# Sums of weight blocks for two Winograd-form products: taken ahead, on POOL, in an earlier stage, and read back from HBM

## Chip, cores and metric

One core of one Trainium2 chip. The metric is the device time of one execution in microseconds, the median of several.

## What is computed

One layer of a hybrid encoder on x (1024 x 1024, float32). The parts that matter here:

```python
h = gate_a * (o_a @ w_branch_a[l]) + gate_b * (o_b @ w_branch_b[l])
x = layer_norm(DEEPNORM_ALPHA * x + h @ w_out[l], ln1_g[l], ln1_b[l])
up = causal_depthwise_conv(x @ w_up[l], conv_ffn[l])
a_ff, b_ff = jnp.split(up, 2, axis=-1)
x = layer_norm(DEEPNORM_ALPHA * x + (jax.nn.silu(a_ff) * b_ff) @ w_down[l], ln2_g[l], ln2_b[l])
```

`o_a` is a gated DeltaNet branch, `o_b` a spatial gating branch; `gate_a` and `gate_b` are sigmoids of columns of `x @ w_in`. w_up is 1024 x 5632, w_down 2816 x 1024.

## The kernel before

Every matrix product is made of three fp32r products of a high and a low part (`TERMS`). `split` (L111) makes the two parts: ScalarE copies the high part (L112), VectorE subtracts it (L113). One matmul is 128x128 by 128x512.

The program runs in stages, as TensorE sees them:

- To about 503 us: input projections, the DeltaNet solve and scan.
- Gate stage, 503 to 717 us: `mixed_b(d)` for d = 3 to 7 (L788), each a gate (L391, 48 matmuls, weights of 512 KB by `load_w`) and a branch (L461, 24 matmuls), then the gate A loop (L809), eight steps of the same size with gates of the next step ahead; `load_wo` brings blocks of w_out (L797). Raw weights go through two buffers (`wr`).
- w_out, 717 to 814 us: per row m of 128 tokens 48 matmuls (`wout_part`), then `wout_end`: residual sum and LayerNorm, whose reciprocal root is on POOL (L245, L246). Rows 0 and 1 are done in two halves of k, so that the blocks k = 4 to 7 are wanted late.
- Transition, 814 to 876 us: first products of the up projection, while the normalised x is transposed by TensorE (`to_b`, four 128x128 transposes to a group) into the operands B[1] to B[7].
- Up stage, 876 to 1280 us: x @ w_up by a Strassen-like scheme in Winograd's form. Columns are taken in 22 groups g of two 128-column blocks; each group has seven products (`up_product`, 12 matmuls). Products 1, 2 and 4 read blocks of w_up as they are; 5, 6, 7 and 3 read sums S of four blocks (`up_sums`, four POOL operations of 128x512, L942). `up_post` makes the convolution and the gating and stores F in HBM (`fd`, L1060). `order` is a fixed list, operands are split `LEAD` = 6 products ahead.
- Down stage, 1280 to 1562 us: F @ w_down by the same scheme, seven products for each of 11 block pairs j. The passes run in the order `PRODS` = 1, 5, 6, 3, 2, 7 (`dn_product`, 12 matmuls per step, L1204), and product 4 at the end from operands that stay in SBUF (L1308). Left sums (of F, `dn_left`, POOL) and right sums (of w_down, `dn_right`, POOL and VectorE in turn, L1156) are made on the way in planes `tt`, `b12`, `b22`, `b21`, `sa` of 11 x 512 columns, which `load_plane` fills from HBM. `finish` normalises and stores rows.

Each engine runs its instructions in the program's order, and SP issues its DMAs in the program's order: a DMA that waits holds up those behind it. Tiles come from pools with a number of buffers; who reuses a buffer waits for its last reader.

## Time and profile before

| | us |
|---|---|
| median of 3 runs | 1570.18 |
| lowest, highest | 1569.42, 1573.58 |
| profiled execution, own time | 1572.81 |
| its span | 1571.1 |
| TensorE busy in it | 1444.5 |
| VectorE busy | 1024.4 |
| ScalarE busy | 548.7 |
| POOL busy | 525.2 |

The profile is of one execution. Busy times are sums over the span; where an engine's idle time lies and what ended it is read from the views below. A DMA-issuing instruction of SP is not counted as busy.

### The profile page before, as it was taken

The page shows a single profiled execution, that of the slowest core. Times are in us where ns is not written, and L with a number is a line of the kernel's source. Part 1 is how long each engine was busy: PE and PEld are TensorE (multiplying, and loading weights), DVE is VectorE, ACT ScalarE, POOL GpSimd, SP SyncE. Part 2 cuts the span into 40 slices and gives each one's busy share as a digit, 9 for nine tenths or more (in the row PEclk, how much of TensorE's full clock was granted, in tenths as well). Part 3 has the DMA queues.
Part 4 walks back from the last instruction along what each step waited for, and adds up shares of the span by engine and source line. Part 5 has one row for each costly group of instructions (what it writes and reads, how often), then busy time and mean ns, then how long its engine had stood idle before and what let it go on. Part 6 is the DMA issues. An engine that isn't in the chain of part 4 may idle for free.

```text
span 1571.1 us, 17995 instructions
## 1 busy us (share of the span) xinstructions
PE 1444.5 (92%) x6807; PEld 1173.2 (75%) x6807; DVE 1024.4 (65%) x1556; ACT 548.7 (35%) x855; POOL 525.2 (33%) x491
## 2 busy tenths in 40 slices
...
POOL 2344353543531000000163233333333104790363
...
GB/s 231 20 36 41 28 15 39 28 27 28 28 14 41 40 54 65 78 60 198 56 67 55 80 81 67 81 84 84 88 68 79 91 153 394 194 121 107 128 100 54
DMA packets 124678, 129.75 MB, mean 83 GB/s; under 512 B 6267, under 2 KB 92975, under 8 KB 124591
## 3 DMA queue, kind: packets, MB, share of 16 engines
...
## 4 chain that ended last, share of the span: by engine, by line
PE 67%; DVE 17%; POOL 5%; DMA 4%; issue 4%; ACT 2%; SPq 0%; POOLq 0%; DVEq 0%; ACTq 0%
PE mm L990 21%; PE mm L391 18%; PE mm L461 6%; PE mm L867 5%; PE sm L990 3%; PE mm L1204 2%; DMA b<-in_w_down_dram 2%; PE sm L1308 2%; PE mm L239 2%; DVE op L113 2%; DVE u L606 2%; PE sm L1204 1%; DVE u L607 1%; DVE y L416 1%; DVE b L113 1%
## 5 line engine op out<-in xcount | busy, mean ns | idle before, releaser
L391 PE MATMUL mm<-xh,wh 128*128 128x512 f32 x1152 | 313.7, 407 | 0.0
L391 PEld LDWEIGHTS mm<-xh,wh 128*128 128x128 f32 x1152 | 213.3, 190 | 40.6 <-issue 0.4
L990 PE MATMUL mm<-xh,op 128*128 128x512 f32 x888 | 218.0, 396 | 6.0 <-DVE ca L1018 4.8
L990 PEld LDWEIGHTS mm<-xh,op 128*128 128x128 f32 x888 | 164.5, 189 | 49.7 <-DVE ca L1018 8.6
L391 PE MATMUL mm<-xh,wl 128*128 128x512 f32 x576 | 160.3, 404 | 0.0
L245 POOL TENSOR_SCALAR rstd<-mv 128x1 f32<-128x1 f32 x24 | 15.9, 662 | 334.5 <-DVE mv L849 310.5
L391 PEld LDWEIGHTS mm<-xh,wl 128*128 128x128 f32 x576 | 106.9, 190 | 20.3
L990 PE MATMUL mm<-xh,wh 128*128 128x512 f32 x348 | 88.4, 400 | 3.7 <-DVE cb L1018 3.2
L113 DVE TENSOR_TENSOR wl<-wr,wh 128x1024 fp32r<-128x1024 f32 x19 | 23.2, 1223 | 96.7 <-PE mm L391 71.1
L990 PE MATMUL mm<-xh,wl 128*128 128x512 f32 x348 | 85.8, 393 | 0.0
L382 POOL TENSOR_TENSOR wl<-wr,wh 128x1024 fp32r<-128x1024 f32 x25 | 60.3, 2412 | 73.5 <-ACT wh L381 21.6
L112 ACT CAST wh<-wr 128x1024 fp32r<-128x1024 f32 (+1 forms) x31 | 27.4, 885 | 154.9 <-PE mm L391 125.6
L990 PEld LDWEIGHTS mm<-xh,wh 128*128 128x128 f32 x348 | 65.0, 191 | 21.5 <-DVE cb L1018 3.6
L1014 DVE SCALAR_TENSOR_TENSOR tb<-cb,cf,tb 128x1023 f32<-128x1023 f32 (+1 forms) x44 | 73.9, 1679 | 4.7 <-ACT tb L1012 3.8
L990 PEld LDWEIGHTS mm<-xh,wl 128*128 128x128 f32 x348 | 64.3, 188 | 16.5 <-DVE ca L1018 1.5
L113 DVE TENSOR_TENSOR op<-ss,op 128x512 fp32r<-128x512 f32 x49 | 46.7, 959 | 31.4 <-ACT op L112 31.4
L1014 DVE SCALAR_TENSOR_TENSOR ta<-ca,cf,ta 128x1023 f32<-128x1023 f32 (+1 forms) x44 | 58.1, 1320 | 13.2 <-ACT ta L1012 12.6
L1204 PE MATMUL sm<-op,op 128*128 128x512 f32 x192 | 49.6, 413 | 13.6 <-DVE op L113 11.5
L112 ACT CAST xh<-sm 128x512 fp32r<-128x512 f32 x44 | 24.3, 589 | 103.7 <-PE sm L895 82.9
L1156 POOL TENSOR_TENSOR tt<-b,tt 128x512 f32<-128x512 f32 x18 | 27.7, 1545 | 96.4 <-DMA b<-in_w_down_dram 86.4
L416 DVE SCALAR_TENSOR_TENSOR y<-mm,cq,y 128x1023 f32<-128x1023 f32 (+2 forms) x36 | 46.0, 1277 | 20.3 <-ACT y L414 20.0
L942 POOL TENSOR_TENSOR ss<-wr 128x512 f32<-128x512 f32 x11 | 15.8, 1432 | 125.6 <-DMA wr<-in_w_up_dram 125.6
...
## 6 DMA issues: line engine op xcount, KB each, us to landing
wr<-in_w_in_dram SPq DMA_DIRECT2D x36, 512.0 KB, 3.9
wr<-fd SPq DMA_DIRECT2D x46, 256.0 KB, 3.0
wr<-in_w_up_dram SPq DMA_DIRECT2D x22, 512.0 KB, 3.9
wq<-in_w_up_dram SPq DMA_DIRECT2D x22, 512.0 KB, 3.9
fd<-ta SPq DMA_DIRECT2D x22, 512.0 KB, 2.6
wq<-fd SPq DMA_DIRECT2D x42, 256.0 KB, 2.9
y<-in_x_dram SPq DMA_DIRECT2D x8, 512.0 KB, 6.9
wr<-in_w_out_dram SPq DMA_DIRECT2D x8, 512.0 KB, 3.7
```

The lines of the kernel that those rows point to most:

```text
L112: nc.scalar.copy(hi, src)
L113: eng.tensor_tensor(out=lo, in0=src, in1=hi.bitcast(F32), op=ALU.subtract)
L239: nc.tensor.matmul(pp[:, 512 * i:512 * i + 260], st, mv[:, 260 * i:260 * i + 260], start=(k, a, b) == (0, 0, 0), stop=(k, a, b) == (KT - 1 ...
L382: nc.gpsimd.tensor_tensor(out=lo, in0=raw, in1=hi.bitcast(F32), op=ALU.subtract)
L391: nc.tensor.matmul(pp[:, half * 512:(half + 1) * 512], w[a][:, k, wcol:wcol + P], act[b][half][:, k], start=n == 0, stop=n == 3 * nk - 1)
L416: nc.vector.scalar_tensor_tensor(out=dst[:, s:], in0=pp[:, :S - s], scalar=taps[n - 1 - s], in1=dst[:, s:], op0=ALU.mult, op1=ALU.add)
L461: nc.tensor.matmul(pp[:, half * 512:(half + 1) * 512], w[a][:, k, wcol:wcol + P], o[k][b][:, half], start=n == 0, stop=n == 11)
L606: nc.vector.tensor_tensor(out=tmp[:, :, :i + 1], in0=LB[:, :, :i + 1, i], in1=x16[:, :, :i + 1], op=ALU.mult)
L867: nc.tensor.matmul(pp[:, nh * 512:(nh + 1) * 512], hT[pair][:, a, k, off:off + P], wo[k][b][:, nh * 512:(nh + 1) * 512], start=k == 0 and ...
L990: nc.tensor.matmul(pp, a[:, i, k * P:(k + 1) * P], b[:, j, k], start=first and n == 0, stop=n == 11, skip_group_check=not first)
L1014: nc.vector.scalar_tensor_tensor(out=dst[:, s:], in0=src[:, :S - s], scalar=cf[:, 2 - s, f:f + 1], in1=dst[:, s:], op0=ALU.mult, op1=ALU.add)
L1204: nc.tensor.matmul(banks[m], a[:, u, m * P:(m + 1) * P], b[:, v], start=first and j == 0 and n == 0, stop=j == NJ - 1 and n == 2, skip_gro ...
```

## The change

Four things, in program order.

1. The small DeltaNet tiles move from pool `sb` to a pool of their own, `dsm`, which is closed when the DeltaNet outputs are split. A pool `pre` takes its place: six buffers of 128x512. In the gate stage, 33 "presums" run through it: 22 for w_up (four blocks loaded, sums 5, 7, 6, 3 on POOL, stored in HBM as `sd`) and 11 for w_down (sums 5, 7, 6, 4 as `td`). Each has four loads and four stores on SP, 256 KB each. Three follow each `mixed_b(d)`, two each step of the gate A loop, the last two `wout_end(1)`.
2. The up stage loads half blocks (256 KB) from `sd` or from w_up, 15 products ahead, and has no POOL sums. The four sums of F that the down products need are taken on VectorE (`f_sums`, 44 operations of 128x512) and stored with the blocks of F, one HBM array for each product (`fd[1]` to `fd[7]`).
3. In the transition, the groups of transposes of T blocks stand between the matmuls of products (0,3), (0,5), (0,6), one group to three matmuls; the post-processing of group 0 is earlier, and row 7 of w_out is in two halves.
4. In the down stage every step loads one block `fd[p][j]` and one `td[p][j]` or block of w_down, and splits both. The planes and their sums are gone; passes run 1, 5, 6, 3, 7, 2, and in passes 7 and 2 the operands of product 4 are split into planes that stay. y comes in over the first eight steps. `finish` of rows 0 to 3 stands behind the last pass.

The core of the diff:

```diff
+    phase["dsm"].close()
+    pre = enter("pre", side="right")
...
+    def presum(kind, n):
+        t = [pre.tile([P, 512], F32, tag="pt", name=name("pt"), bufs=6) for _ in range(4)]
+        if kind == "S":
+            a11, a12, a21, a22 = t
+            for d, i in ((a21, 0), (a22, 4), (a11, 1), (a12, 2)):
+                nc.sync.dma_start(v3(d, 4), up_block(n, i))
+            todo = ((a22, a21, a22, ALU.add, 5), (a21, a11, a21, ALU.subtract, 7), (a11, a22, a11, ALU.subtract, 6),
+                    (a12, a12, a11, ALU.subtract, 3))
+        else:
+            b11, b12, b21, b22 = t
+            for d, i in ((b11, 1), (b12, 0), (b22, 3), (b21, 2)):
+                nc.sync.dma_start(d, dn_block(n, i))
+            todo = ((b11, b12, b11, ALU.subtract, 5), (b12, b22, b12, ALU.subtract, 7),
+                    (b22, b22, b11, ALU.subtract, 6), (b21, b21, b22, ALU.subtract, 4))
+        for o, p, q, op, i in todo:
+            nc.gpsimd.tensor_tensor(out=o, in0=p, in1=q, op=op)
+            nc.sync.dma_start((sd if kind == "S" else td)[i][n], o)
...
     for d in range(len(hraw), 8):
         run(mixed_b(d))
+        some_presums(3)
...
         nc.vector.tensor_tensor(out=hraw[d], in0=hraw[d], in1=sA[d], op=ALU.add)
+        some_presums(2)
...
     wout_end(pp1, 1)
+    some_presums(len(presums))
...
-    def block_product(pp, a, b, first=False):
+    def block_product(pp, a, b, first, between=()):
         n = 0
         for i, j in TERMS:
             for k in range(4):
+                if n % 3 == 0 and between:
+                    to_b(*between.pop(0))
...
+    def f_sums(j):
+
+        f0, f1 = G[2 * j]["ta"], G[2 * j + 1]["ta"]
+        s1, s2, s3, s4 = (left.tile([P, 512], F32, tag="fs", name=name("fs"), bufs=4) for _ in range(4))
+        for i, o, a, b, op in ((5, s1, f0[:, H1], f1[:, H1], ALU.add), (6, s2, s1, f0[:, H0], ALU.subtract),
+                               (7, s3, f0[:, H0], f0[:, H1], ALU.subtract), (3, s4, f1[:, H0], s2, ALU.subtract)):
+            plus(o, a, b, op)
+            nc.sync.dma_start(fd[i][j], o)
+            yield
...
+    for pos, i in ((4, 6), (5, 7), (6, 4)):
         if i == 4:
             phase["act1"].close()
             new_b(4, enter("right2", side="right"), "xh3", 1)
...
+        ahead(pos - 3)
+        up_product(*order[pos], between=[(i, m, trow[m][i]) for m in range(4, NT)])
+        up_post(*order[pos])
...
-    PRODS = (1, 5, 6, 3, 2, 7)
+    PRODS = (1, 5, 6, 3, 7, 2)
...
     def dn_load(p, j):
         t = new_raw()
...
+        nc.sync.dma_start(t[:, H0], fd[p][j])
+        nc.sync.dma_start(t[:, H1], td[p][j] if p in td else dn_block(j, p))
         raw[p, j] = t
...
     def dn_ops(p, j):
         t = raw.pop((p, j))
...
+        if p == 4:
+            split(hiA[:, j], loA[:, j], t[:, H0])
+            split(hiW[:, j], loW[:, j], t[:, H1])
+            return
```

How the order of instructions moves, at three places: SP's queue twice, TensorE once.

SP in the gate stage, before. `wr` are raw weights; from w_in 512 KB for a gate, from w_branch for a branch. `wr_716` is the gate of d = 5.

```order
L379 DMA wr_701_4458<-in_w_in_dram 128x8x128
L379 DMA wr_707_4541<-in_w_in_dram 128x8x128
L379 DMA wr_712_4598<-in_w_branch_b_dram 128x4x256
L379 DMA wr_716_4630<-in_w_in_dram 128x8x128
L379 DMA wr_722_4713<-in_w_in_dram 128x8x128
L379 DMA wr_727_4770<-in_w_branch_b_dram 128x4x256
L379 DMA wr_731_4802<-in_w_in_dram 128x8x128
L379 DMA wr_737_4885<-in_w_in_dram 128x8x128
L379 DMA wr_742_4942<-in_w_in_dram 128x8x128
```

SP at the same place, after. `pt` are the presums' tiles, `wr_740` is the gate of d = 5.

```order
L814 DMA pt_732_4709<-in_w_up_dram 128x4x128
L814 DMA pt_733_4710<-in_w_up_dram 128x4x128
L814 DMA pt_738_4727<-in_w_up_dram 128x4x128
L825 DMA sd5_4466<-pt_735_4712 128x512
L825 DMA sd7_4468<-pt_734_4711 128x512
L825 DMA sd6_4467<-pt_732_4709 128x512
L825 DMA sd3_4465<-pt_733_4710 128x512
L814 DMA pt_739_4728<-in_w_up_dram 128x4x128
L814 DMA pt_736_4725<-in_w_up_dram 128x4x128
L814 DMA pt_737_4726<-in_w_up_dram 128x4x128
L381 DMA wr_740_4741<-in_w_in_dram 128x8x128
L825 DMA sd5_4466<-pt_739_4728 128x512
```

Ahead of the gate load now stand the four stores of presum 4 (counted from 0) and loads of presum 5; of the two inputs of that presum's first sum, one (`pt_738`) is issued ahead of these stores and the other (`pt_739`) behind them.

SP at the end of the gate stage, before: the last loads of w_out (L797, 512 KB; the last four are k = 4 to 7) and then w_up's.

```order
L379 DMA wr_786_5365<-in_w_branch_a_dram 128x4x256
L797 DMA wr_789_5371<-in_w_out_dram 128x1024
L379 DMA wr_793_5404<-in_w_in_dram 128x8x128
L379 DMA wr_799_5488<-in_w_in_dram 128x8x128
L379 DMA wr_804_5545<-in_w_branch_a_dram 128x4x256
L797 DMA wr_813_5673<-in_w_out_dram 128x1024
L797 DMA wr_816_5679<-in_w_out_dram 128x1024
L797 DMA wr_819_5685<-in_w_out_dram 128x1024
L797 DMA wr_822_5691<-in_w_out_dram 128x1024
L932 DMA wr_865_6094<-in_w_up_dram 128x8x128
L932 DMA wr_866_6096<-in_w_up_dram 128x8x128
```

SP at the same place, after: the blocks of w_out for k = 5, 6 and 7 (`wr_940`, `wr_943`, `wr_946`) and the loads and stores of the last three presums.

```order
L825 DMA td4_4469<-pt_931_6102 128x512
L844 DMA wr_940_6190<-in_w_out_dram 128x1024
L820 DMA pt_967_6360<-in_w_down_dram 128x512
L820 DMA pt_968_6361<-in_w_down_dram 128x512
L820 DMA pt_970_6363<-in_w_down_dram 128x512
L820 DMA pt_969_6362<-in_w_down_dram 128x512
L820 DMA pt_971_6376<-in_w_down_dram 128x512
L825 DMA td5_4470<-pt_967_6360 128x512
L825 DMA td7_4472<-pt_968_6361 128x512
L844 DMA wr_943_6196<-in_w_out_dram 128x1024
L825 DMA td6_4471<-pt_970_6363 128x512
L844 DMA wr_946_6202<-in_w_out_dram 128x1024
```

The four loads of w_out, which stood in a row, are now each behind one or more stores of a presum.

On POOL, all operations of the presums stand ahead of the reciprocal roots of LayerNorm of rows 0 and 1, which before came right after the weights' splits.

TensorE in the transition, before: groups of four transposes (`sm<-ident,y8`, L895) and up products (L990).

```order
L990 MATMUL sm_907_6440<-xh_856_6037,op_891_6344 128x512 x12
L895 MATMUL sm_908_6453<-ident_105,y8_831_5716 128x128 x4
L895 MATMUL sm_909_6460<-ident_105,y8_832_5718 128x128 x4
L895 MATMUL sm_910_6467<-ident_105,y8_833_5720 128x128 x4
L895 MATMUL sm_911_6474<-ident_105,y8_896_6355 128x128 x4
L895 MATMUL sm_912_6481<-ident_105,y8_831_5716 128x128 x4
L895 MATMUL sm_913_6488<-ident_105,y8_832_5718 128x128 x4
L895 MATMUL sm_914_6495<-ident_105,y8_833_5720 128x128 x4
L895 MATMUL sm_915_6502<-ident_105,y8_896_6355 128x128 x4
L895 MATMUL sm_917_6514<-ident_105,y8_827_5708 128x128 x4
L895 MATMUL sm_918_6521<-ident_105,y8_828_5710 128x128 x4
L895 MATMUL sm_919_6528<-ident_105,y8_829_5712 128x128 x4
```

TensorE at the same place, after: transposes are L940, products L1057.

```order
L1057 MATMUL mm_1029_6915<-xh_1017_6876,op_1040_7007 128x512 x3
L940 MATMUL sm_1051_7075<-ident_108,y8_956_6229 128x128 x2
L1057 MATMUL mm_1029_6915<-xh_1017_6876,op_1040_7007 128x512 x3
L940 MATMUL sm_1052_7085<-ident_108,y8_957_6231 128x128 x4
L1057 MATMUL mm_1029_6915<-xh_1017_6876,op_1040_7007 128x512 x3
L940 MATMUL sm_1053_7095<-ident_108,y8_1028_6910 128x128 x4
L1057 MATMUL mm_1029_6915<-xh_1017_6876,op_1040_7007 128x512 x3
L940 MATMUL sm_1057_7116<-ident_108,y8_951_6219 128x128 x4
L940 MATMUL sm_1058_7126<-ident_108,y8_952_6221 128x128 x4
L940 MATMUL sm_1059_7136<-ident_108,y8_953_6223 128x128 x4
L1057 MATMUL mm_1029_6915<-xh2_1018_6877,op_1042_7013 128x512 x9
L940 MATMUL sm_1060_7146<-ident_108,y8_954_6225 128x128 x4
```

The groups of transposes that stood in a row are now between three matmuls each.

## Rows read from the trace of the kernel before

**Rows 1.** The page's 40 equal slices of the span, POOL's busy share in tenths.

```profile
POOL 2344353543531000000163233333333104790363
```

**Rows 2.** Busy time of each engine by stretch (sum in us, share of instructions recorded), then the granted clock as a share of full speed, the DMA engines' mean busy share and what they moved. The stretches are the gate stage, the transition, the up stage, the down stage, and of the latter 1300 to 1350.

```profile
503.00:720.00 217.00, 217.00 (x950) 178.06 (x949) 62.76 (x73) 47.01 (x65) 0.00 (x0) 1.00 0.20 59
...
814.00:876.00 62.00, 46.70 (x202) 36.03 (x202) 42.26 (x52) 26.87 (x45) 27.47 (x20) 0.89 0.20 60
876.00:1280.00 404.00, 399.18 (x1725) 317.90 (x1724) 308.55 (x310) 192.68 (x286) 124.42 (x72) 1.00 0.26 84
1280.00:1562.50 282.50, 227.41 (x916) 177.95 (x915) 204.19 (x219) 91.52 (x148) 138.71 (x110) 0.92 0.46 162
...
1300.00:1350.00 50.00, 23.61 (x79) 16.98 (x80) 30.72 (x32) 8.40 (x15) 28.73 (x19) 0.77 0.98 367
```

**Rows 3.** Waits of all engines in the down stage, by the operation that waited and what ended it: us in total, times, the longest.

```profile
POOL tt L1156 <- DMA b<-in_w_down_dram: 86.4, 4, 75.6
...
ACT wl L112 <- DMA tt<-in_w_down_dram: 20.7, 1, 20.7
```

**Rows 4.** TensorE's timeline in the down stage, at its two longest gaps: start, us, instruction, and in brackets the idle time before it and what ended that.

```profile
1311.65 0.79 PE L1204 MATMUL sm<-wl,wh 128*128 128x512 f32 x1 [11.72 <-ACT wl L112]
...
1504.25 6.85 PE L1204 MATMUL sm<-op,op 128*128 128x512 f32 x22 [9.85 <-DVE op L113]
```

**Rows 5.** POOL's timeline in the transition: sums of 128x512 with VectorE at other work (818 to 821) and not (841 to 846).

```profile
817.90 2.15 POOL L942 TENSOR_TENSOR ss<-wr,ss 128x512 f32<-128x512 f32 x1
820.01 1.71 POOL L942 TENSOR_TENSOR ss<-wr,wr 128x512 f32<-128x512 f32 x1
...
840.79 1.28 POOL L942 TENSOR_TENSOR ss<-wr 128x512 f32<-128x512 f32 x1 [7.80 <-DMA wr<-in_w_up_dram]
...
844.72 1.27 POOL L942 TENSOR_TENSOR ss<-wr,wr 128x512 f32<-128x512 f32 x1
```

**Rows 6.** POOL's and SP's timelines near the end, where SP stores what POOL has summed (two halves each), and the page's list of DMA issues (KB each, median us to landing).

```profile
1553.30 2.53 POOL L1232 TENSOR_TENSOR y<-y,lt 128x512 f32<-128x512 f32 x2 [2.62 <-DVE y L1229]
...
1554.61 1.58 SPq L1233 DMA_DIRECT2D out_dram<-y  x2
...
wr<-in_w_in_dram SPq DMA_DIRECT2D x36, 512.0 KB, 3.9
wr<-fd SPq DMA_DIRECT2D x46, 256.0 KB, 3.0
```

**Rows 7.** SP's timeline at one gate load of 512 KB, ScalarE's at the cast that it released, and VectorE's at the end of the DeltaNet stage.

```profile
515.83 0.37 SPq L379 DMA_DIRECT2D wr<-in_w_in_dram  x1
...
519.24 1.05 ACT L112 CAST wh<-wr 128x1024 fp32r<-128x1024 f32 x1 [3.69 <-PE mm L461]
...
489.33 1.22 DVE L113 TENSOR_TENSOR kv<-y,kv 128x1024 fp32r<-128x1024 f32 x1
```

**Rows 8.** VectorE's groups in the gate stage, 503 to 720: count, busy us, mean ns, idle before.

```profile
L113 DVE TENSOR_TENSOR wl<-wr,wh 128x1024 fp32r<-128x1024 f32 x18 | 22.0, 1223 | 90.4 <-PE mm L391 64.7 <-ACT wh L112 25.6
...
L113 DVE TENSOR_TENSOR xh<-y,xh 128x256 fp32r<-128x256 f32 x28 | 9.8, 421 | 3.1 <-ACT xh L112 3.1
L818 DVE TENSOR_TENSOR y<-y,y 128x1024 f32<-128x1024 f32 x7 | 8.6, 1222 | 0.1
```

**Rows 9.** What SP's queue waited for from 500 to 720: us in total, times, the longest.

```profile
SPq L379 <- DVE wl L113: 109.4, 13, 16.1
```

**Rows 10.** TensorE's timeline at the first matmuls of two gates in a row.

```profile
503.42 3.81 PE L391 MATMUL mm<-xh,wh 128*128 128x512 f32 x16
...
519.93 3.81 PE L391 MATMUL mm<-xh,wh 128*128 128x512 f32 x16
```

**Rows 11.** TensorE's timeline in w_out, the first use of the block for k=7 (`xx`).

```profile
730.83 0.85 PE L867 MATMUL mm<-xx,xh 128*128 128x512 f32 x3
```

**Rows 12.** TensorE's timeline in the transition.

```profile
826.12 2.82 PE L895 MATMUL sm<-ident,y 128*128 128x128 f32 x12 [5.78 <-DVE y L857]
...
832.60 1.16 PE L895 MATMUL sm<-ident,y 128*128 128x128 f32 x8 [0.18 <-DVE xh L113]
833.70 2.55 PE L990 MATMUL sm<-xh,op 128*128 128x512 f32 x10
...
868.61 4.61 PE L990 MATMUL mm<-xh,wh 128*128 128x512 f32 x12 [3.22 <-DVE cb L1018]
```

**Rows 13.** VectorE's groups in the up stage, 900 to 1280.

```profile
L1014 DVE SCALAR_TENSOR_TENSOR tb<-cb,cf,tb 128x1023 f32<-128x1023 f32 (+1 forms) x38 | 64.4, 1694 | 3.9 <-ACT tb L1012 3.1
L1014 DVE SCALAR_TENSOR_TENSOR ta<-ca,cf,ta 128x1023 f32<-128x1023 f32 (+1 forms) x40 | 51.3, 1282 | 12.3 <-ACT ta L1012 11.8
L113 DVE TENSOR_TENSOR op<-ss,op 128x512 fp32r<-128x512 f32 x40 | 39.3, 986 | 28.3 <-ACT op L112 28.3
...
L113 DVE TENSOR_TENSOR op<-wr,op 128x512 fp32r<-128x512 f32 x18 | 12.3, 685 | 3.2 <-ACT op L112 3.1
```

**Rows 14.** TensorE's timeline in a dense part of the down stage, two products of 12 matmuls.

```profile
1420.71 2.88 PE L1204 MATMUL mm<-op,op 128*128 128x512 f32 x12
1423.43 2.88 PE L1204 MATMUL mm<-wh,op 128*128 128x512 f32 x12
```

**Rows 15.** POOL's sums in the up stage by shape and operands, the first (largest) and last of 8 groups, 68 sums in all.

```profile
L942 POOL TENSOR_TENSOR ss<-wr,wr 128x512 f32<-128x512 f32 x8 | 16.7, 2082 | 2.5 <-DVE wh L113 1.3 <-DVE wl L113 0.6 <-DVE op L113 0.6
...
L942 POOL TENSOR_TENSOR ss<-wr 128x512 f32<-128x512 f32 x8 | 11.4, 1428 | 98.3 <-DMA wr<-in_w_up_dram 98.3
```

345 lines of the change are left out of this document (150 added, 195 removed).

## The prediction

> **What bounds the kernel now.** I read the page's 40 slices first, then the busy times by stage, and then, for each stage that the diff touches, what ends TensorE's waits there. POOL is idle for six slices in the middle [rows 1]; by stage that is the gate stage, 503 to 720 us, where POOL runs nothing, TensorE fills the window (217.00 of 217.00), the DMA engines are used to 0.20, and VectorE to 62.8/217 = 29% [rows 2]. So work put there is free if TensorE's own operands keep coming. Two later stretches are not bound by TensorE: the transition (814 to 876) has 46.7 us of matmul in 62.0, and the down stage (1280 to 1562.5) 227.4 in 282.5, both at a lower granted clock, 0.89 and 0.92 [rows 2]. In the down stage the longest waits are POOL's for w_down (86.4 us) and ScalarE's (20.7) [rows 3]; they reach TensorE as gaps of 11.72 and 9.85 us, the second behind VectorE [rows 4]. At 1300 to 1350 the DMA share is 0.98: planes of w_down, F blocks and y all come at once [rows 2]. The up stage is nearly dense. The change spends time in the first stretch to save it in the others.
>
> **Gate stage: the presums' period.** Each presum is four loads and four stores of 256 KB on SP and four POOL sums of 128x512; 33 of them. SP runs its queue in program order, and the second input of the first sum (a22, or the matching T block) of presum n+1 is issued behind the last store of presum n, which waits for the last POOL sum. So the presums form one chain, and its period is T = 4 sums + POOL to SP + one issue + one landing.
> The sums: four of the same shape run from 840.79 to 844.72 + 1.27, 5.20 us in all, with VectorE not in the way [rows 5]. POOL's end at about 1553.30 + 1.27 to SP's next issue at 1554.61 is 0.04; the issue itself is 0.37 [rows 6, 7]. Landing of 256 KB: the page gives 3.0 in a loaded stage [rows 6]; 512 KB alone came from the issue at 515.83 to the cast that it released at 519.24 in 3.4 [rows 7]. I take 2.6, nearer to the second, since this stage's DMA share is low. That is 8.2. Beside VectorE operations with two SBUF inputs a sum took 2.15 and 1.71 in place of 1.28 [rows 5]; in this stage such operations fill about 48 us of 217 (18 x 1.22, 28 x 0.42, 7 x 1.22 and smaller ones [rows 8]), 22%. 5.2 x 0.22 x 0.68 = 0.8 if each sum meets its share; 0.6 taken. **T = 8.8 us** (8.0 with landing 2.3 and few collisions, 9.4 with landing 2.9 and all of them).
> SP's loads have slack now: the gate loads wait 109.4 us for a free buffer, up to 16.1 at a time [rows 9], and 0.37 per issue would cost nothing. But TensorE takes 16.51 us per gate (503.42 to 519.93 [rows 10]), while the change lets only one gate load through per three presums in the first loop, 3T = 26.4, and one per two, 2T = 17.6, in the second. What is queued behind the waiting store on SP is thus the next weight, and TensorE waits for that.
> Times: the small tiles are free when VectorE ends its splits, about 490 [rows 7]; presum 0 ends at about 499, presum n at 499 + 8.8n. Gate d=5 is behind the stores of presum 4 (534.2) and three loads (1.1): landed 3.4 later and cast in 1.05, 540, where TensorE wants it at 536.4: 3.6 lost. Gates 6 and 7 and the first gate A come 26.4 apart, each 9.9 later than TensorE needs: 33 us lost by then. In the second loop 17.6 against 16.5 loses 1 per step, mostly covered by loads that are ahead. The last four w_out blocks stand behind presums 29 to 31. The block for k=7 goes out after the third sum of presum 31, 499 + 8.8 x 31 - 1.3 = 770.5; with issue 0.4, landing 3.4 and the two splits 2.3 it is 776.6. The weight loads between presums add up to 24 x 0.37 = 9 where they stand ahead of a chain load. Before, TensorE used that block at 730.83 [rows 11]. 776.6 - 730.8 = 46, up to 55. After a 9.85 us gap 22 matmuls took 6.85 us against 5.0 at the dense rate [rows 4, 14], 1.9 per gap, part of it under the next wait. **Cost: +55 (35 to 80).** One us more of T costs about 32, because some 31 periods stand ahead of that block.
> POOL's LayerNorm steps of rows 0 and 1 stand behind all the sums (presum 32 ends at about 790); TensorE then has w_out row 2 (48 matmuls, 11 us) and its sums in a PSUM buffer of its own, so I cost that at nothing; if it shows, a few us.
> [...]
>
> **Transition.** The transposes of T blocks (to_b) go from twelve groups in a row to one group per three matmuls. TensorE's waits there were 5.78 us before the first group, behind VectorE's normalisation (L857), and 3.22 on VectorE's sums [rows 12]. Busy 46.7 less what the clock took, 62.0 x 0.11 = 6.8, leaves 40 [rows 2]; eight transposes at full clock take 1.10 (832.60 to 833.70) [rows 12], so 80 of them 11, and these are in the 40. The 5.78 remains in part, since the same row 7 ends last, though the order now has to_b of row 4 to 6 and two whole products ahead of to_b(3,7). I keep 7 of the 22 us: 47. **-15 (-8 to -20).**
>
> **Up stage.** POOL's sums go, and with them the slow VectorE operations: tb 1694 ns against ta's 1282, op<-ss 986 against op<-wr 685 [rows 13]; VectorE gains some 46 us and pays 44 sums x 0.68 = 30 for F. TensorE's window is 404.0 us for 1725 matmuls; at the dense rate, 12 in 2.72 (1420.71 to 1423.43 [rows 14]), 391. VectorE has 76% of the time filled, so it can only make short waits. Bounds: all 13 gained, or 6 lost if the seven half-block loads per group (1.8 MB in 18 us, 100 GB/s, against 367 reached [rows 2]) come late. **-4 (-10 to +6).**
>
> **Down stage.** Every step now takes one 256 KB F block and one w_down or T block, made ready long before, and four splits: no POOL sum, no plane. 916 matmuls at 0.2267 are 207.7 [rows 2, 14]. VectorE does 2 x 0.685 of 2.72 per step, in passes 7 and 2 six per two steps (4.1 of 5.4): below one. DMA: 512 KB per 2.72 us is 193 GB/s, in passes 7 and 2 half as much again (289), in the first eight steps with y 386, where 367 was the mean of the full stretch [rows 2]; so the first eight steps may lose 2 to 3 us, and with the first splits and six pass ends I put 8 on top: 216. **-66 (-55 to -74).** Late next is VectorE in passes 7 and 2. The tail of 8.7 us stays: the last rows' sums still follow the last product.
>
> **Sum.** Span 1571.1, own time 1572.8: +55 - 15 - 4 - 66 = -30, 1542.8. The median lies 2.6 under the profiled run, 1570.2, so **1541**; with T from 8.0 to 9.4 and the other bounds 1518 to 1565.
>
> **Rivals.** (A) The presums hide entirely: each sum's loads are ahead and T is at most 5.5, a third of 16.5. Then D is 0 to 5 and the time 1488. Against it: the store-then-load order on one queue; four sums alone take 5.2. For it: six buffers, so that one of the two inputs is early.
> (B) Slower: VectorE and POOL shut each other out in the gate stage, and TensorE gets its weights still later. At the up stage's mean of the eight forms of sum (2082 the longest, 1428 the shortest, mean 1.73 [rows 15]) four take 6.9, with landing 2.9 T = 10.2, cost 55 + 1.4 x 32 = 100, time 1586; with 3.9 of landing [rows 6] 1618. It decides from T = 9.8, where the cost is 85, all that the other stages give. Against it: VectorE is used to 29% here and 76% there [rows 2]. [...]
> (C) The down stage gives only half, since 256 KB blocks arrive singly with eight steps' worth of buffers and the transfers of two engines' queues meet at its start: -33 in place of -66, 1574. Against it: the DMA share outside 1300 to 1350 was far from full.
>
> **How the numbers follow.** Forecast 0.68; A 0.06; something between A and the forecast 0.04; B 0.15; C 0.07. What this kernel's measurement can tell from no change is 0.3%, 4.7 us: C falls mostly within it, some of the forecast's upper end too. Faster 0.77, same 0.08, slower 0.15. The range 1510 to 1576 holds the forecast, the part below it and C, and leaves out A and most of B.
>
> **What would show it.** In the profile after: TensorE waits of 3 to 10 us ahead of the matmuls of gates 5, 6, 7 and the first gate A, put down to ScalarE or VectorE splits behind a DMA; POOL busy in groups of four sums with 2.5 to 3.5 us between them, 8.8 us apart; the last w_out block at 780 to 790. Transition of 45 to 50, up stage of 395 to 405, down stage of 210 to 220 with a granted clock near 1. If TensorE has no gaps in the gate stage, A is right; if the groups are 10 us apart or more, B; if the down stage still has gaps before VectorE splits that wait for DMA, C.

## The result

The changed kernel takes 1591.46 us, median of 4 runs (1588.30 to 1593.43), the kernel before 1571.88 (1569.42 to 1574.67): a ratio of 1.0122, 95% interval 1.0096 to 1.0148. It is slower, by 1.2% or some 20 us; the forecast was 1541, and 1576 was the end of its range.

Both profiled executions, cut at the same places of TensorE's order of instructions (the tail is the time after the last matmul; the lines add up to the span within 0.5 us):

| stage | before, us | after, us | difference | forecast |
|---|---|---|---|---|
| up to w_out's first matmul | 717.5 | 791.4 | +73.9 | } +55 |
| w_out | 96.5 | 127.8 | +31.3 | } |
| transition | 62.0 | 41.2 | -20.8 | -15 |
| up stage | 403.6 | 399.2 | -4.4 | -4 |
| down stage | 282.4 | 207.5 | -75.0 | -66 |
| tail | 8.7 | 19.1 | +10.4 | 0 |
| span | 1571.1 | 1586.6 | +15.5 | -30 |

So the later stages gave 100 us, 15 more than forecast; the gate stage and w_out took 105 in place of 55, and 10 came back at the end.

The page of the changed kernel: slices of the busy share of TensorE, POOL and the DMA engines, and DMA landings (KB, median us from issue to landing); between them POOL's sums of the presums (count, busy us, mean ns, idle before).

```profile
PE   8999999989899675987939999999999999999995
...
POOL 2354353534525555444643320000000000000016
...
DMA  7111101010106777787685154444444444776822
...
L824 POOL TENSOR_TENSOR pt<-pt,pt 128x512 f32<-128x512 f32 x132 | 184.8, 1400 | 169.8 <-DMA pt<-in_w_up_dram 82.6
...
pt<-in_w_up_dram SPq DMA_DIRECT2D x88, 256.0 KB, 4.3
sd<-pt SPq DMA_DIRECT2D x88, 256.0 KB, 2.1
```

POOL, which was idle in six slices [rows 1], is now busy there by a half, and the DMA engines are at 7 to 8 tenths. TensorE, which was full there, falls to between 5 and 9 tenths. In the up stage and most of the down stage POOL is idle and TensorE full.

Windows of the changed kernel, for the stages of the table (gate stage, w_out, transition, up, down, tail; columns as in [rows 2]).

```profile
503.00:791.40 288.40, 227.80 (x927) 183.44 (x926) 64.70 (x65) 43.06 (x59) 152.24 (x110) 0.88 0.76 237
791.40:919.20 127.80, 100.09 (x429) 78.74 (x428) 59.66 (x77) 15.17 (x27) 53.63 (x45) 0.88 0.48 171
919.20:960.40 41.20, 39.44 (x202) 31.73 (x201) 34.16 (x51) 25.64 (x43) 4.93 (x4) 1.00 0.48 153
960.40:1360.00 399.60, 399.60 (x1729) 318.38 (x1728) 286.69 (x353) 192.97 (x288) 0.00 (x0) 1.00 0.44 143
1360.00:1567.40 207.40, 207.23 (x912) 170.64 (x911) 129.01 (x202) 88.72 (x151) 21.23 (x32) 1.00 0.63 215
1567.40:1586.60 19.20, 0.03 (x1) 0.00 (x0) 8.84 (x11) 2.48 (x2) 8.60 (x13) 0.61 0.26 96
```

The down stage is at TensorE's rate: 207.23 busy of 207.40 and a clock of 1.00, against 227.41 of 282.50 and 0.92 [rows 2]; TensorE waits there once, for 0.2 us, and the waits of [rows 3] are gone. VectorE there fell from 204 to 129 us. The gate stage is no longer full: 227.80 busy of 288.40, at a clock of 0.88. Its 73.9 us more are 60.6 of idle time and 13.3 of longer busy time for the same matmuls (214.5 before).

TensorE's timeline in the changed kernel: the first matmuls of gates 5, 6, 7 and the first gate A, then two places in w_out (the gap in brackets, and what ended it).

```profile
547.50 5.57 PE L393 MATMUL mm<-xh,wh 128*128 128x512 f32 x16 [14.11 <-ACT y L472]
...
574.74 5.60 PE L393 MATMUL mm<-xh,wh 128*128 128x512 f32 x16 [8.98 <-ACT wh L114]
...
604.25 6.16 PE L393 MATMUL mm<-xh,wh 128*128 128x512 f32 x16 [11.21 <-ACT wh L114]
...
632.88 5.55 PE L393 MATMUL mm<-xh,wh 128*128 128x512 f32 x16 [9.78 <-ACT wh L114]
...
806.97 7.37 PE L915 MATMUL mm<-ob,xh 128*128 128x512 f32 x24 [9.90 <-DVE y L864]
...
834.69 0.63 PE L915 MATMUL mm<-xx,xh 128*128 128x512 f32 x1
```

The gaps of 9 to 14 us ahead of these four gates are the ones that the prediction named; with four smaller ones of 3 to 5 us behind them they make up the 60.6. Gate 5 came at 547.5 where 540 was forecast, the first gate A at 632.9 (619). The block for k = 7 of w_out is used at 834.69, where 776 to 785 was forecast and 730.83 was before [rows 11].

POOL's timeline in the changed kernel: groups of four sums, each one presum.

```profile
532.39 5.31 POOL L824 TENSOR_TENSOR pt<-pt,pt 128x512 f32<-128x512 f32 x4 [3.79 <-DMA pt<-in_w_up_dram]
541.46 5.29 POOL L824 TENSOR_TENSOR pt<-pt,pt 128x512 f32<-128x512 f32 x4 [3.76 <-DMA pt<-in_w_up_dram]
551.46 5.39 POOL L824 TENSOR_TENSOR pt<-pt,pt 128x512 f32<-128x512 f32 x4 [4.71 <-DMA pt<-in_w_up_dram]
...
643.33 6.25 POOL L824 TENSOR_TENSOR pt<-pt,pt 128x512 f32<-128x512 f32 x4 [10.27 <-DMA pt<-in_w_up_dram]
653.52 5.41 POOL L824 TENSOR_TENSOR pt<-pt,pt 128x512 f32<-128x512 f32 x4 [3.94 <-DMA pt<-in_w_up_dram]
665.25 6.73 POOL L824 TENSOR_TENSOR pt<-pt,pt 128x512 f32<-128x512 f32 x4 [6.33 <-DMA pt<-in_w_up_dram]
```

Between two presums with no weight between (532.39 to 541.46) the period is 9.1; sums take 5.3, and 3.8 lie between. Across a weight's load it is 10.0 (541.46 to 551.46), and in the second loop, where a gate, a branch and a w_out block stand in two presums, 10.2 and 11.7. From the first presum (starting at 492.79) to the last (834.62) 32 periods make 341.8 us, 10.7 each; 8.8 was forecast.

SP's timeline at the load of the gate for d = 5 (a piece is several DMAs in a row).

```profile
533.70 4.34 SPq L825 DMA_DIRECT2D sd<-pt  x4
538.09 1.59 SPq L814 DMA_DIRECT2D pt<-in_w_up_dram  x3
539.78 0.45 SPq L381 DMA_DIRECT2D wr<-in_w_in_dram  x1
```

The four stores of presum 4 are issued one by one as POOL ends its sums (533.70 to 538.04), then three loads, 0.53 us each and not 0.37, and only then the gate (539.78). Its own landing grew too: the 11 gate loads from 500 to 780 took 5.7 us (median) from issue to landing, where the page of before has 3.9 [rows 6].

### The profile page after: what moved, and what is told of

The parts are those of the page before. It is cut to its first block, busy times and chain, and to the rows that moved or that the text cites. A ratio compares the mean times of both kernels' runs of the same rounds, so it can differ in the third digit from the quotient of the medians.

```text
span 1586.6 us, 18921 instructions
## 1 busy us (share of the span) xinstructions
PE 1440.9 (91%) x6807; PEld 1175.1 (74%) x6807; DVE 934.6 (59%) x1587; ACT 548.6 (35%) x863; POOL 452.3 (29%) x467
## 4 chain that ended last, share of the span: by engine, by line
PE 42%; POOL 3%; DVE 2%; DMA 1%; issue 1%; ACT 1%; SPq 0%; POOLq 0%; DVEq 0%
PE mm L1057 23%; PE mm L1232 6%; PE sm L1232 6%; PE mm L915 4%; PE sm L1057 3%; POOL y L1259 1%; POOL pt L824 1%; PE sm L940 1%; DMA pt<-in_w_down_dram 1%; DMA wr<-in_w_out_dram 0%; POOL y L950 0%; ACT y L1267 0%; POOL rstd L248 0%; DVE y L1256 0%; DVE y L905 0%
## 5 line engine op out<-in xcount | busy, mean ns | idle before, releaser
L393 PE MATMUL mm<-xh,wh 128*128 128x512 f32 x1152 | 329.0, 423 | 60.6 <-ACT y L472 30.6
L393 PEld LDWEIGHTS mm<-xh,wh 128*128 128x128 f32 x1152 | 223.3, 200 | 108.4 <-ACT y L472 33.6
L824 POOL TENSOR_TENSOR pt<-pt,pt 128x512 f32<-128x512 f32 x132 | 184.8, 1400 | 169.8 <-DMA pt<-in_w_up_dram 82.6
L1057 PE MATMUL mm<-xh,op 128*128 128x512 f32 x888 | 219.9, 395 | 0.2 <-ACT cb L1134 0.2
L247 POOL TENSOR_SCALAR rstd<-mv 128x1 f32<-128x1 f32 x24 | 15.1, 631 | 679.0 <-DVE mv L897 654.9
L1057 PEld LDWEIGHTS mm<-xh,op 128*128 128x128 f32 x888 | 162.5, 188 | 42.8 <-DVE ca L1086 3.0
L393 PE MATMUL mm<-xh,wl 128*128 128x512 f32 x576 | 163.2, 410 | 0.0
L115 DVE TENSOR_TENSOR op<-wq,op 128x512 fp32r<-128x512 f32 x95 | 64.2, 686 | 49.8 <-ACT op L114 49.8
L1057 PE MATMUL mm<-xh,wl 128*128 128x512 f32 x348 | 87.1, 394 | 1.5 <-ACT p L1115 1.5
L1057 PE MATMUL mm<-xh,wh 128*128 128x512 f32 x348 | 85.6, 393 | 0.0
L114 ACT CAST op<-wq 128x512 fp32r<-128x512 f32 x95 | 57.8, 621 | 65.3 <-PE mm L1057 29.5
L1057 PEld LDWEIGHTS mm<-xh,wl 128*128 128x128 f32 x348 | 63.9, 188 | 18.5 <-ACT p L1115 2.8
L1057 PEld LDWEIGHTS mm<-xh,wh 128*128 128x128 f32 x348 | 64.1, 188 | 16.6 <-DVE ca L1086 1.2
L1082 DVE SCALAR_TENSOR_TENSOR tb<-cb,cf,tb 128x1023 f32<-128x1023 f32 (+1 forms) x44 | 56.4, 1282 | 12.2 <-ACT tb L1080 11.8
L915 PE MATMUL mm<-ob,xh 128*128 128x512 f32 x192 | 48.6, 403 | 9.9 <-DVE y L864 9.9
L115 DVE TENSOR_TENSOR op<-wr,op 128x512 fp32r<-128x512 f32 x65 | 43.7, 686 | 20.0 <-ACT op L114 16.8
```

Of the source, the lines that this page charges most:

```text
L114: nc.scalar.copy(hi, src)
L115: eng.tensor_tensor(out=lo, in0=src, in1=hi.bitcast(F32), op=ALU.subtract)
L393: nc.tensor.matmul(pp[:, half * 512:(half + 1) * 512], w[a][:, k, wcol:wcol + P], act[b][half][:, k], start=n == 0, stop=n == 3 * nk - 1)
L824: nc.gpsimd.tensor_tensor(out=o, in0=p, in1=q, op=op)
L915: nc.tensor.matmul(pp[:, nh * 512:(nh + 1) * 512], hT[pair][:, a, k, off:off + P], wo[k][b][:, nh * 512:(nh + 1) * 512], start=k == 0 and ...
L1057: nc.tensor.matmul(pp, a[:, i, k * P:(k + 1) * P], b[:, j, k], start=first and n == 0, stop=n == 11, skip_group_check=not first)
```

## Experiments

All times of the experiments stand beside a kernel before of 1569 to 1576 us on the same chip. Each is a single run unless a median is given. The runs of one kernel lie 5 to 10 us apart, so smaller differences are read from the windows of the stages and not from the time. The first four ask what makes the cost in the gate stage.

### No presums at all

```diff
-        some_presums(3)
...
-            nc.sync.dma_start(t, sd[i][g])
+            nc.sync.dma_start(v3(t, 4), up_block(g, {5: 0, 7: 4, 6: 1, 3: 2}.get(i, i)))
```

> Left out: all 33 presums (loads, sums, stores); products read a plain block of w_up or w_down in place of each stored sum, so every transfer and split of the later stages stays. Chain theory (the presums' queue order delays TensorE's weights by 105 us in the gate stage and w_out): time 1591 - 105 = 1486, between 1478 and 1495, w_out's first matmul back at 715 to 718, later stages unchanged. Rival (part of the 105 us is the new pools or the earlier closing of the DeltaNet tiles): above 1500.

1481.16 us. Windows of the gate stage and w_out:

```profile
503.00:715.00 212.00, 212.00 (x933) 174.74 (x932) 59.38 (x71) 46.32 (x65) 0.00 (x0) 1.00 0.20 58
715.00:812.00 97.00, 94.87 (x429) 77.45 (x428) 53.58 (x72) 12.41 (x22) 28.09 (x26) 0.98 0.32 114
```

TensorE is full in the gate stage again, w_out starts at 714.9. The presums cost 107 to 110 us (by the spans, 1586.6 - 1479.4, and by the times, 1591.5 - 1481.2), and nothing else of the change costs anything before the transition. The later stages are as in the change: 41.2, 399.1 and 207.5.

### Sums without transfers

```diff
+        a, b, c, d = rt
+        for o, p, q in ((a, b, a), (b, c, b), (c, d, c), (d, a, d)):
+            nc.gpsimd.tensor_tensor(out=o, in0=p, in1=q, op=ALU.subtract)
```

> Left out: the presums' loads and stores; POOL makes the same 132 sums of 128x512 on four resident tiles, back to back from about 490 us, products read plain blocks as in the run without presums. Chain theory: TensorE never waits for POOL, time within 3 us of the run without presums (about 1486), sums 1.30 to 1.45 us each. Rival (POOL and VectorE exclude each other for whole instructions): with POOL always busy the weight splits on VectorE are late, sums 1.6 us and more, time 15 us or more above the run without presums.

1483.19 us, 2 more than without presums. POOL's 132 sums (busy us, mean ns), the gate stage's window, and then one split of a weight on VectorE and one sum on POOL that met it:

```profile
L813 POOL TENSOR_TENSOR pt<-pt,pt 128x512 f32<-128x512 f32 x132 | 194.3, 1472 | 10.3
```

```profile
503.00:715.00 212.00, 212.00 (x932) 174.81 (x932) 76.25 (x66) 43.72 (x59) 184.67 (x126) 1.00 0.21 60
```

```profile
548.87 2.35 DVE L115 TENSOR_TENSOR wl<-wr,wh 128x1024 fp32r<-128x1024 f32 x1 [9.64 <-PE mm L393]
...
550.22 2.15 POOL L813 TENSOR_TENSOR pt<-pt,pt 128x512 f32<-128x512 f32 x1
```

POOL worked for 184.67 us of these 212 beside VectorE, and TensorE never waited (212.00 busy of 212.00). The two engines do lengthen each other's instructions. The split takes 1.22 us by itself [rows 8]; here it took 2.35, until 551.22. The sum that began at 550.22 took 2.15, where one takes 1.28 by itself [rows 5], and ended 1.15 after the split. The trace of the changed kernel shows the same many times: 15 of its 132 sums began during VectorE's split of a weight or its addition of a whole row (L865), took 1.37 to 2.31 us and ended 1.13 to 1.15 after that instruction, while the 92 sums that met no VectorE instruction took 1.26 to 1.30. And ten splits of a weight there began during a sum, took 1.27 to 2.28 us and ended 1.08 after it. VectorE was busy for 76.25 us against 59.38 with POOL idle. But TensorE waits for none of it in this stage. Rival B of the prediction, as the cause of the cost, is out.

### Transfers without sums

```diff
         for o, p, q, op, i in todo:
-            nc.gpsimd.tensor_tensor(out=o, in0=p, in1=q, op=op)
             nc.sync.dma_start((sd if kind == "S" else td)[i][n], o)
```

> Left out: the 132 sums; all loads and stores stay, a store waits only for the load of its tile. Chain theory: the period loses the 5.3 us of sums, to 4 to 5.5, under the 5.5 that TensorE allows in the first loop; the gate stage loses 0 to 10 us, time 1486 to 1500. Rival (the transfers themselves, or HBM, are short): the period stays above 7 and time above 1515.

1518.71 us, between the two: 73 less than the change, still 38 more than without presums. The DMA engines in 500 to 620:

```profile
500.00:620.00 120.00, 102.45 (x412) 82.78 (x411) 17.03 (x15) 13.52 (x13) 0.00 (x0) 0.90 1.00 300
```

They are full, at 300 GB/s. Without sums the transfers themselves are the limit: the groups of four stores began 6.5 to 7.6 us apart where no weight stood between them, 8.4 on average. The forecast of 4 to 5.5 failed here, and the rival's words (a period above 7, a time above 1515) came true: a second limit lies not far below the first, at about 7 us.

### The first pair of inputs a presum ahead

```diff
-            for d, i in ((a21, 0), (a22, 4), (a11, 1), (a12, 2)):
-                nc.sync.dma_start(v3(d, 4), up_block(n, i))
...
+            if k == 1:
+                load_pair(at + 1, 1)
+        load_pair(at + 2, 0)
```

> Same loads, sums and stores; each presum's first two inputs are issued a whole presum earlier, ahead of the stores of the presum before, so that the first sum follows the last one at once and only the second sum waits behind the stores. Chain theory: the period falls from 9.7 to 7.7 to 8.2 in the first loop, cost falls by 32 us for each us, to 40 to 60, time 1525 to 1550. Rival (POOL and VectorE shut each other out, or HBM is short): sums and landings grow as they come denser, period stays above 9, time above 1575.

1561.13 us, 30 less than the change, though less of a gain than expected. POOL:

```profile
545.98 5.16 POOL L851 TENSOR_TENSOR pt<-pt,pt 128x512 f32<-128x512 f32 x4 [2.61 <-issue]
555.01 5.29 POOL L851 TENSOR_TENSOR pt<-pt,pt 128x512 f32<-128x512 f32 x4 [3.87 <-issue]
562.82 5.27 POOL L851 TENSOR_TENSOR pt<-pt,pt 128x512 f32<-128x512 f32 x4 [2.52 <-issue]
570.30 5.23 POOL L851 TENSOR_TENSOR pt<-pt,pt 128x512 f32<-128x512 f32 x4 [2.22 <-issue]
581.50 5.25 POOL L851 TENSOR_TENSOR pt<-pt,pt 128x512 f32<-128x512 f32 x4 [5.96 <-issue]
```

Two presums with no weight between are now 7.5 to 7.8 us apart (555.01, 562.82, 570.30), with one between 9.0 and 11.2; over all 32 periods the average fell from 10.7 to 9.3. So the order on SP does make part of the period, and these sums did not grow (5.2 to 5.3). The average is still above the 7.7 to 8.2 that the theory gave. Of the rival's words (sums and landings grow, a period above 9), the landings around the weights came true, and with them the average.

### Weights on ScalarE's queue

```diff
-        nc.sync.dma_start(v3(raw, a), srcs[0])
+        (nc.sync if pool_lo[0] else nc.scalar).dma_start(v3(raw, a), srcs[0])
...
-        nc.sync.dma_start(raw, wosrc[k])
+        nc.scalar.dma_start(raw, wosrc[k])
```

> All presums as in the change; the loads of gate, branch and w_out weights in the gate stage are issued by ScalarE's queue, so that they no longer stand behind the presums' stores on SP. Queue theory: TensorE's gaps in the gate stage go, w_out's first matmul is back at 715 to 725; the presums themselves still take 9 to 10 us each and end at about 800, and POOL's LayerNorm steps of rows 0 and 1 stand behind them, so the cost moves there: w_out ends 40 to 70 us late, time 1525 to 1550. Rival (the weights are late because the transfers are slow under the presums' traffic): gate stage still 20 us or more late with the same gaps, time above 1560.

1583.25 us; w_out starts at 818, later than in the change. The queue theory fell. The rival's numbers came true (a gate stage over 20 us late, a time above 1560), but the reason is another. ScalarE's timeline:

```profile
568.61 0.38 ACTq L381 DMA_DIRECT2D wr<-in_w_in_dram  x1
569.08 1.04 ACT L114 CAST wh<-wr 128x1024 fp32r<-128x1024 f32 x1 [22.15 <-DMA pt<-in_w_up_dram]
```

ScalarE stood for 22 us before it issued a gate's load at 568.61, and what came last was a presum's load (five such waits make 84.4 us). So on ScalarE's queue, too, weights went out behind transfers of the presums, and here ScalarE's casts and sigmoids waited behind them as well. What makes a load on ScalarE's queue wait for one on SP's, no run shows.

### Only the sums of w_down in the gate stage

```diff
-    presums = [("S", g) for g in range(NF)] + [("T", j) for j in range(NF // 2)]
+    presums = [("T", j) for j in range(NF // 2)]
...
+        s1, s2, s4, s3 = (rs.tile([P, 512], F32, tag="ss", name=name("ss"), bufs=6) for _ in range(4))
+        for o, a, b, op in ((s1, G[g]["a21"], s[4], ALU.add), (s2, s1, s[1], ALU.subtract),
```

Two raw buffers fewer and two F tiles fewer made room in SBUF.

> Only the 11 presums of w_down in the gate stage, one for each of 11 steps; the sums of w_up are made on POOL in the up stage as in the kernel before; transition and down stage as in the change. Queue theory: a period of 10 to 11 us is under the 16.5 us of a step, so the gate stage costs 0 to 8 us; the up stage gives back its 4 us; time 1481 + 4 + 0 to 8, 1483 to 1500. Rival (any presum between two weights costs its own wait, wherever it stands): 11 of 33 presums cost a third of 105, time 1515 to 1525.

1534.90 us against 1572.57. Windows of gate stage, transition, up and down stage:

```profile
503.00:723.50 220.50, 211.17 (x919) 173.51 (x918) 61.73 (x70) 45.87 (x65) 53.02 (x38) 0.98 0.46 145
...
819.20:870.90 51.70, 42.55 (x202) 33.53 (x201) 42.47 (x51) 26.67 (x45) 27.23 (x20) 0.93 0.24 69
870.90:1295.00 424.10, 407.62 (x1730) 321.81 (x1730) 338.81 (x351) 190.93 (x286) 126.32 (x72) 0.99 0.31 99
1295.00:1514.20 219.20, 209.86 (x912) 172.57 (x910) 131.35 (x204) 90.56 (x153) 21.32 (x32) 0.98 0.62 208
```

TensorE's longest wait in the up stage (us in total, times, the longest), and VectorE's normalisation of row 7 in the transition:

```profile
PE mm L1065 <- DVE ca L1094: 15.1, 9, 3.5
...
827.83 3.43 DVE L905 SCALAR_TENSOR_TENSOR y<-y,rstd,wh 128x512 f32<-128x512 f32 x2 [2.09 <-POOL rstd L248]
```

The gate stage costs 9 us against none without presums, in one gap of 9.33: that part went as expected. The rest did not: transition 51.8 (41.2), up stage 423.7 (399.2), down 219.2 (207.5). What came back with the w_up sums is largely VectorE's time beside POOL. In the transition the two halves of row 7's normalisation took 3.43 us (1.40 in the change), ahead of the longest gap of TensorE there, 5.9. In the up stage VectorE was busy for 338.81 us (286.69 in the change, with two instructions more) and TensorE waited 15.1 for it; it waited for nothing in the change, where POOL's sums are gone, and 4.8 in the kernel before, where VectorE does not have F's sums. The fewer buffers may carry part of the 11 and 24, which this run doesn't part. So what cost nothing in the gate stage, where VectorE has slack (61.73 us busy of 220.50), does cost where VectorE is nearly full (338.81 of 424.10). The time of 1535 came close to the rival's number, for another reason than the rival's.

### Two per step

```diff
         run(mixed_b(d))
-        some_presums(3)
+        some_presums(2)
...
-    some_presums(len(presums))
+    some_presums(2)
...
+        if m < NT - 1:
+            some_presums(1)
```

> The change with the same spreading (two per step, two after row 1, one after rows 2 to 6) and its own order of loads. Period 9.5 to 11 makes 19 to 22 us per step against 16.5: theory says 13 steps lose 30 to 70 us, w_out 5 to 15, time 1520 to 1560. Rival (the bunching of three in the first loop made the cost, two per step are absorbed): under 1510.

1578.74 us: 13 less than the change; w_out starts at 779.6. Taken alone the ratio gives little, since the period stays what it was and the w_out stage gets presums too (129.8 us). Above the range's end by 19.

With the pairs ahead as well:

> All 33 presums, each first pair issued a presum ahead as in the run with pairs ahead, and spread: two after every step of the gate stage (26), two after row 1 of w_out and one after each of rows 2 to 6. One weight per two presums: a period of 7.9 to 8.5 makes 15.8 to 17 us per step against TensorE's 16.5. Theory (what counts is presums per weight times period): gate stage 0 to 15 us late, w_out 0 to 10 us longer, time 1481 + 5 to 25, 1486 to 1506. Rival (each presum ahead of a weight costs its own wait, whatever the ratio): 33 presums still cost 60 us or more, time above 1540.

1537.36 us against 1568.94. The gate stage loses 32 us against the run without presums and w_out 24; the cost is 56, which is above what the theory gave and 3 us under the rival's bound of 1540. Period times number goes in the right direction, but the transfers of 26 presums do not hide in 13 steps: the DMA share is 0.85 to 0.91 there.

### Pieces of 1 KB

```diff
+    def up_pair(u, i):
+        g, h = 2 * (u // 2), u % 2
...
-                nc.sync.dma_start(v3(d, 4), up_block(n, i))
+                nc.sync.dma_start(v3(d, 2), up_pair(n, i))
```

> The change, with a presum of w_up taken over two neighbouring groups and half of the rows: the same 256 KB per load, sum and store, read in pieces of 1 KB in place of 512 B (the up stage reads the sums back in two loads of 128 KB). The DMA engines were 0.77 to 0.80 busy at 240 GB/s in the gate stage, 0.98 at 300 GB/s in the run without sums. Theory (landing of 3.4 to 4.2 us in place of the forecast 2.6 comes from the engine time of small pieces): landing 2.6 to 3.2, period 9.7 to 8.8 in the first loop, share 0.65 to 0.7, cost 20 to 35 us less, 1555 to 1572. Rival (landing is a fixed time of a load on a busy queue): landing stays near 3.4 to 4.2, time 1583 to 1593.

1599.87 us: no gain. The DMA share fell from 0.77 to 0.69 in 500 to 560, but 4.0 to 4.8 us lay between two presums' sums in place of 3.8. So the engines' time on small pieces is not what makes the landing longer than forecast. What does stays open.

### No gate and branch weights in the queue

```diff
+        if kept and not pool_lo[0]:
+            hi, lo = kept[-1]
+            a = srcs[0].shape[1]
+            return v3(hi, a), v3(lo, a)
```

> Left out: all loads of gate and branch weights in the gate stage (every gate and branch uses the weights loaded last before it); the eight w_out blocks and all presums stay. Theory (the period is 9.1 us where no weight stands between two presums, and each 512 KB weight adds about 2 us to it on the same queue, which the forecast put at 0.37): periods of 9.0 to 9.3 except at the w_out blocks, the last presum ends at 795 to 810 in place of 841, w_out's last block comes 55 to 70 us late, time 1535 to 1555. Rival (the period grows by itself under load, from 9.1 to 10 or 11, whatever is between): the last presum at 825 or later, time above 1570.

1572.70 us. The time missed, since TensorE stood for 52 us at one place (the first w_out block came behind 21 presums on SP, and VectorE's product waited behind its split), but the period can be read:

```profile
639.23 5.30 POOL L831 TENSOR_TENSOR pt<-pt,pt 128x512 f32<-128x512 f32 x4 [3.93 <-DMA pt<-in_w_up_dram]
648.38 5.28 POOL L831 TENSOR_TENSOR pt<-pt,pt 128x512 f32<-128x512 f32 x4 [3.84 <-DMA pt<-in_w_up_dram]
657.56 5.28 POOL L831 TENSOR_TENSOR pt<-pt,pt 128x512 f32<-128x512 f32 x4 [3.90 <-DMA pt<-in_w_up_dram]
```

9.2 here; from the first presum (495.68) to the last (805.30) 9.7 on average, against 10.7 with the weights. 1.0 x 32 = 32 us go to the 17 loads that stand between these presums in the change, 1.9 us each, as the theory had it. The other half of the difference from 8.8 is there without them, so the rival had a part too.

### LayerNorm's and x's loads on SP

In the changed kernel ScalarE's timeline around the start of w_out was:

```profile
802.06 0.41 ACTq L877 DMA_DIRECT2D wh<-in_ln_g_dram  x1
802.51 0.71 ACT L114 CAST xh<-y 128x256 fp32r<-128x256 f32 x2 [17.61 <-DMA pt<-in_w_down_dram]
```

Its casts for the last operands of w_out (802.51) stood behind the load of LayerNorm's weights, a stall of 17 us (785 to 802), and what came last was a presum's load.

```diff
-    nc.scalar.dma_start(lnp[0], ln1_g[0].partition_broadcast(P))
+    nc.sync.dma_start(lnp[0], ln1_g[0].partition_broadcast(P))
...
-        nc.scalar.dma_start(yt, xin[m])
+        nc.sync.dma_start(yt, xin[m])
```

> The change, with the loads of LayerNorm's weights and of x at the start of w_out moved from ScalarE's queue to SP's. [...] If that stall makes w_out longer (127.8 us against 96.5 before): w_out 108 to 118, time 10 to 20 us less, 1571 to 1581. Rival (the last w_out blocks behind the presums' stores make it, the stall is covered): w_out 122 to 130, time within 5 us of 1591.

1583.98 us; w_out 121.4 against 127.8. It lies between the two: the gap of 9.90 is gone, and of that 6 us show. In its place TensorE now waits 9.3 us for the cast of a w_out block, whose load landed late behind the presums.

### Transposes in a row

```diff
-        up_product(*order[pos], between=[(i, m, trow[m][i]) for m in range(4, NT)])
+        for m in range(4, NT):
+            to_b(i, m, trow[m][i])
+        up_product(*order[pos])
```

> The change, with the groups of transposes of T blocks in a row ahead of their product in place of one to three matmuls. If the interleaving is what took the transition from 62.0 to 41.2 us: 48 to 56 us. Rival (the earlier post-processing and the loads that no longer wait for POOL took it): 41 to 44.

The transition took 39.0 us, less than with them between the matmuls:

```profile
923.80:962.80 39.00, 38.82 (x202) 31.70 (x201) 34.27 (x52) 25.60 (x43) 3.68 (x3) 1.00 0.51 161
```

So the interleaving did not bring the 20.8 us. In the run with only the w_down sums, with POOL's sums back, 10.6 of them were lost again (51.8), though that run has fewer buffers too; the rest goes to the other edits of that stretch, which were not parted.

### The tail

POOL's timeline at the end of the changed kernel (L1259 are the last additions, L247 a row's reciprocal root):

```profile
1547.36 12.85 POOL L1259 TENSOR_TENSOR y<-y,lt 128x512 f32<-128x512 f32 x8 [1.31 <-issue]
1560.29 0.19 POOL L247 TENSOR_SCALAR rstd<-mv 128x1 f32<-128x1 f32 x1
...
1566.98 0.19 POOL L247 TENSOR_SCALAR rstd<-mv 128x1 f32<-128x1 f32 x1
```

Eight additions of rows 0 to 3 run for 12.85 us, and row 4's root stands behind them, at 1560.29; from there each row takes 6.7 us one after the other.

```diff
-            nc.gpsimd.tensor_tensor(out=y[m][:, hs], in0=y[m][:, hs], in1=lt[:, 1, hs], op=ALU.add)
+            eng.tensor_tensor(out=y[m][:, hs], in0=y[m][:, hs], in1=lt[:, 1, hs], op=ALU.add)
```

> The change, with the last additions of rows 0 to 3 (eight of 128x512) on VectorE in place of POOL. Theory (the tail grew from 8.7 to 19.1 us because POOL's eight additions in a row hold up the reciprocal roots of rows 4 to 7 behind them): tail after the last matmul 8 to 10 us, time 9 to 11 us less, 1580 to 1583. Rival (the tail grew because a row's chain is longer than a row's products whatever is ahead): tail stays above 16.

1590.02 us; the tail fell from 19.1 to 14.3, not to 9: the same work then stood ahead of row 4's sums on VectorE. So the order of passes was undone:

```diff
-    PRODS = (1, 5, 6, 3, 7, 2)
+    PRODS = (1, 5, 6, 3, 2, 7)
...
+            if p == 2:
+                for m in range(4):
+                    finish(m)
```

> The change, with pass 2 ahead of pass 7 and the normalisation of rows 0 to 3 right after pass 2, as the kernel before has it. Theory (the tail grew because the work of rows 0 to 3 runs beside the last products, on POOL and VectorE, and holds up rows 4 to 7): tail 8 to 10 us in place of 19.1, a wait of 1 to 3 us for the sums of pass 7 ahead of the last products, time 6 to 10 us less, 1581 to 1586. Rival (the tail has another cause, the loads or splits of product 4): above 15.

1587.52 us. Windows of the down stage and the tail:

```profile
1359.40:1577.40 218.00, 209.53 (x912) 171.59 (x911) 140.11 (x208) 90.84 (x153) 30.62 (x42) 0.98 0.62 208
1577.40:1585.80 8.40, 0.00 (x0) 0.00 (x0) 4.29 (x6) 0.00 (x0) 2.74 (x3) 0.68 0.34 125
```

The tail is 8.4, as before, and the down stage 218.0 in place of 207.5. So the work of rows 0 to 3 beside the last products did make the tail. The 6 to 10 us less that were expected did not come: what the change's order saves in the passes it gives back in the tail, to within 1 us.

### What is left together

> All of it together: pairs loaded ahead, two presums per step and one per row of w_out, pieces of 1 KB, and the last additions of rows 0 and 2 on VectorE. If period and DMA share are what remains: gate stage 5 to 20 us late, w_out 5 to 15 us longer than 97, tail 3 to 6 us shorter, 1500 to 1525, faster than both kernels by 3 to 5% against the kernel before. Rival (what remains of the cost in the run with pairs and spreading, 56 us, is the order of weights on SP): 1525 to 1540.

1532.43 us, median of 4 (1526.65 to 1536.20), against 1573.07: ratio 0.9747, interval 0.9718 to 0.9777. Windows of the gate stage and w_out:

```profile
503.00:741.10 238.10, 216.24 (x923) 175.86 (x921) 73.02 (x65) 42.67 (x59) 139.44 (x104) 0.96 0.86 278
741.10:858.80 117.70, 99.85 (x429) 79.28 (x430) 61.45 (x77) 15.09 (x27) 57.82 (x49) 0.91 0.56 198
```

> Pairs loaded ahead, two presums per step and one per row of w_out, pieces of 512 B as in the change, and pass 2 ahead of pass 7. If the parts add up: the 1537 of the run with pairs and spreading less 7 to 10 for the tail, 1525 to 1532, 0.968 to 0.976 of the kernel before. Rival (the passes' order costs in passes what it saves in the tail): 1533 to 1540.

1535.58 us, median of 4 (1529.10 to 1539.86), ratio 0.975, interval 0.972 to 0.978. The two do not differ beyond their intervals, and both are faster than both kernels; the run with only the w_down sums, 1534.90 once, is as fast. In the first of the two the gate stage still takes 26 us more than without presums, at a DMA share of 0.86, and w_out 21. Both times fell into the rival's range: for the first, that the order of weights on SP is what remains (1525 to 1540), which no run parts from the high DMA share; for the second, that the passes' order costs what it saves (1533 to 1540), as the run before had shown.

## Why the prediction was wrong

The sign came out wrong by one term: **the cost of the gate stage and w_out, 105 us where 55 (35 to 80) stood**. The way in which the cost arises was right: the run without presums gave 110 back, the gaps lie ahead of the gates that were named, and another order of the same loads gave 30. The sums cost by their place in the chain (73 less without them) and not by their work beside VectorE (2 us). The step that failed is the period T = 8.8 us, which was 10.7. Over 32 periods that is 61 us, of which TensorE shows 50.

- Of its parts, the sums held: 5.3 to 5.4 in most of the first loop, up to 6.7 and once 10.4 later, 5.6 on average (184.8 us for 33 presums), against 5.8. The landing did not: it was 3.3 to 3.4 (3.8 between two presums less the store's issue and the signal from POOL) and not 2.6, so that two presums in a row are 9.1 apart, and 9.7 on average without the weights. No row gives 2.6. I leaned on 3.4 us for a single load of 512 KB, and that was misread: the cast at 519.24 waited for TensorE, as its bracket says [rows 7], and was of an earlier load; the page has 3.9 for such loads and 3.0 for the smaller ones [rows 6]. And the low DMA share, my reason for the low value, was that of the kernel before, 0.20; with the presums it is 0.76.
- The weights' loads entered the period at their issue time, 0.37 us each. They cost 1.9 each on the presums' chain, 32 us of the 61 for 17 loads of gate and branch weights. That they share the DMA engines with the chain's loads, at 0.76, is the likely reason, and no run shows it apart. Issue itself was 0.53 for a presum's load, not 0.37.
- Above T = 9.8 the prediction had rival B decide, at a cost of 85. The number held (10.7 gave 105; 55 + 1.9 x 32 = 116), but by luck, for the mechanism of B did not: VectorE and POOL do lengthen each other's instructions, and TensorE does not wait for it here: with POOL busy for 185 us it lost none. And my reading of [rows 5] was wrong, that beside VectorE a sum takes longer by a share of its own time, 0.68. The one at 817.90 met an instruction that ran until 818.90, and ended 1.15 after that, as the sums of the changed kernel that began during a split do (1.13 to 1.15). Nor was VectorE idle beside the sums of 841 to 846, which took 1.27 to 1.28: it ran splits with one input from `sm`. Once a sum was held by a whole row of splits (it began at 785.27 and took 5.26 us); collisions were few, and on average they made the 0.4 us by which a presum's sums exceeded 5.20, where 0.6 had been taken.
- A term that was missing: a LayerNorm load on ScalarE that stood 17 us for a presum's transfer, 6 us of w_out. I had looked at SP and POOL alone. Nor was a term there for the gate loads' own landing, 5.7 us in place of 3.4, which adds to the lateness of gate 5.
- TensorE's granted clock was 0.88 in the gate stage, where it had been 1.00 [rows 2]. Its busy time rose from 214 to 228 us with the same matmuls: 13 of the stage's 74 us. This term was sized rightly: after a gap the first 16 matmuls of a gate took 5.6 us (547.50) against 3.81 [rows 10], 1.8 for each long gap where 1.9 stood.

The gains: transition -20.8 (forecast -15), up stage -4.4 (-4), down stage -75.0 (-66); the last is at the dense rate and has no first-step loss, so the 8 us put on top were too many. The transition came out just beyond the end of its range (-20), and by luck: the reason given was not it, since transposes in a row do as well. "The tail of 8.7 us stays" was wrong, by 10.4: finish of rows 0 to 3 was put beside the last products without asking what on POOL and VectorE stands behind it.

Rival A (presums hidden) and C (half a gain in the down stage) are both out.
